# One core, attention and convolution in a decoder trunk: inverse root by logarithm and exponential, queries 512 wide, and the projection's weight subtractions one tile later

## The chip, the cores and the metric

The kernel runs on one core of one Trainium2 chip. The core has TensorE (PE, matrix products), VectorE (DVE), ScalarE (ACT), GpSimd (POOL) and the sync engine (SP), which here issues DMAs only; each works through its own list of instructions, and they wait for each other by semaphores. The metric is the device time of one execution in microseconds (us), as a median of runs.

## The reference

A trunk of two layers on 256 positions of width 1024. Each layer is half an FFN, a mixer, half an FFN; the mixer of layer 0 is a gated short convolution, that of layer 1 sparse attention with three branches on a shared K/V.

```python
def swiglu_ffn(x, w_in, w_out):
    gate, up = jnp.split(x @ w_in, 2, axis=-1)
    return (jax.nn.silu(gate) * up) @ w_out

def short_conv_mixer(x, w_in, conv_w, w_out):
    b_gate, c_gate, v = jnp.split(x @ w_in, 3, axis=-1)
    u = c_gate * v
    y = depthwise_causal_conv(u, conv_w)             # width 3
    return (b_gate * y) @ w_out

def nsa_mixer(x, w_q, q_norm, w_o, rel_bias, kv):
    proj = x @ w_q
    q = rmsnorm(proj[..., :1024] as 16 heads of 64, q_norm)
    gates = sigmoid(proj[..., 1024:])                # 3 per head
    # per head: o_c (compressed blocks), o_s (selected blocks), o_w (window), each
    # softmax(q @ k.T / 8 + rel_bias[bucket]) @ v with its own keys and mask
    out = gates[0] * o_c + gates[1] * o_s + gates[2] * o_w
    return out @ w_o

for i in range(2):
    if i == 1: kv = shared_kv(h, ...)
    h = h + 0.5 * swiglu_ffn(rmsnorm(h, ffn1_norm[i]), ...)
    h = h + mixer(rmsnorm(h, mix_norm[i]))
    h = h + 0.5 * swiglu_ffn(rmsnorm(h, ffn2_norm[i]), ...)
```

## The kernel before

**Split arithmetic.** Every product is made from halves: an operand is copied to a rounded type (its high half) and the rest is found by subtraction (its low half); high x high, high x low and low x high are added up in PSUM. For weights the class `Stream` does this. It loads 1 MB chunks by SP into `ws` (3 buffers); `high()` casts 1024 columns into `wh` on ACT (L148) and keeps them on a list; `low()` takes the oldest from that list and subtracts into `wl` on VectorE (L165). A unit (`wh`, `wl`) is free again after `done()`; six may be held. A chunk has two units, and a `ws` buffer is loaded anew when the low half of its second unit has been made.

**Stages.** The hidden state `h` lies in SBUF as 8 tiles of 128 x 256 (inside `base`). In turn come: FFN, convolution, FFN, K/V, FFN, attention, FFN. An FFN's first product works in groups of two column tiles: 16 matmuls of 512 columns (L322), then 16 of 256 (L325), from the inputs `xs`.

**The convolution's output projection** is `out_proj(zs, 1.0, nm)` with 8 input tiles, so its evacuation `out_evac` takes the `short` way. For each of the 8 output tiles c TensorE makes a product into one of 4 PSUM banks `a` (tiles 0 to 3 by L322/L325, tiles 4 to 7 by L434/L436); then VectorE adds it to `h[c]` (L394, twice), ACT scales it into the high half of the next stage's input (`norm.high`, L276), ACT squares it (`norm.squares`, L291) for POOL to add up (L293), and VectorE makes its low half (`norm.low`, L280), one tile later. Between them stand `W.high()` and `W.low()`, which prepare weights to come. After them follows the first group of the next FFN: tiles 0 to 5 of `xs`, then tile 6, then the row sums of the norm (L298, on the added squares), then tile 7.

**Attention** runs over 8 pairs of heads j, each with two heads g. The string `ORDER` is a program written out by hand: each word calls one function of the table `ops`, and each engine gets its instructions in the order of the words. `S_j` makes the scores (L1009) into both `mm` banks, `M_j_g` adds the bias and takes minima on VectorE (L1017), `E_j_g` exponentials on ACT (L1028), `R` reciprocals on VectorE, `N` the scaling on POOL (with `_d` on VectorE), `T` and `H` transposes on TensorE into a bank `a`, `C` and `CH` copies out of it on ACT (with `_d` on VectorE), `V_j` the product with the values and the compressed branch's weights, `O` and `P` its halves, `CM` to `CPC` the compressed branch, `WA` and `WD` weights' high and low halves, `WO` the output projection.

Queries come in two parts. Those of heads 0 to 7 are made ahead of the words. The later ones (`F`, 16 words) are made between the words as filler. In the kernel before they are two lots of 256 columns, q = 2 and 3; each is squared (`SQ`), summed and scaled (`RD`), brought to an inverse root by a bit trick and three Newton steps on VectorE (`NW`, L913 to L918), multiplied (`QM`), transposed (`QT`) and scaled (`QC`).

Of the kernel before, what the change touches and what calls it, by code (L numbers as in the profile page):

```python
# [44 lines left out]
F E_0_1 R_0_1 SQ_2 F RD_2 S_1 QT_1 E_0_0 F F QC_1 R_0_0 M_1_0 N_0_1 M_1_1 E_1_0 F S_2 NW_2 N_0_0 F CM_0 CX_0 F F E_1_1
R_1_0 N_1_0 CE_0 M_2_1 CR_0 QM_2 F E_2_1 R_1_1 CG_0 T_0_1 T_0_0 H_0 M_2_0 R_2_1 SQ_3 C_0_1 N_1_1_d E_2_0 S_3 QT_2
C_0_0 CI_0 N_2_1 CH_0_d CL_0 R_2_0 T_1_1 M_3_1 M_3_0 QC_2 C_1_1 T_2_1 CM_1 T_1_0 C_2_1 H_1 N_2_0 E_3_0 RD_3 CX_1 CH_1
C_1_0 CP_0 CPC_0 NW_3 S_4 CE_1 R_3_0 T_2_0 M_4_0 CR_1 N_3_0 M_4_1 CG_1 H_2 C_2_0 V_0 E_3_1 R_3_1 V_1 QM_3 E_4_0 R_4_0
# [11 lines left out]
def trunk(ctx, tc, A, out):  # L60
# [331 lines left out]
    def out_evac(o, c, factor, norm, short=False):  # L392
        for x in range(2):
            ve.scalar_tensor_tensor(out=h[c], in0=o[:, x * T:(x + 1) * T], scalar=factor, in1=h[c], op0=ALU.mult, op1=ALU.add)  # L394
# [498 lines left out]
    def q_reduce(q, tt, w):
        n = w // 64
        s = X["s"] if q == 0 else X.setdefault(("s", q), sm([P, 8])) if tt == 0 else X["s", q]
        ve.tensor_reduce(out=s[:, tt * n:tt * n + n], in_=X.pop(("sq", q, tt)).rearrange("p (n d) -> p n d", d=64), axis=AX.X, op=ALU.add)
        if tt:
            for a in range(2):
                z = s[:, a * n:a * n + n]
                ve.tensor_scalar(out=z, in0=z, scalar1=1.0 / 64, scalar2=X["s"][:, 18 + a:19 + a], op0=ALU.mult, op1=ALU.add)  # L900
# [8 lines left out]
    def q_newton(q):  # L909

        x = X.pop(("s", q))
        y, t = sm([P, 8]), sm([P, 8])
        ve.tensor_scalar(out=y.bitcast(I32), in0=x.bitcast(I32), scalar1=1, scalar2=None, op0=ALU.logical_shift_right)  # L913
# [7 lines left out]
    def q_normed(q, tt, w):  # L921

        n = w // 64
        X["q", q, tt] = t = t2([P, w])
        r = X["r", q][:, tt * n:tt * n + n].rearrange("p (g a) -> p g a", g=2)[:, :, :, None].to_broadcast([P, 2, n // 2, 64])
        ve.tensor_tensor(out=t.rearrange("p (a g d) -> p g a d", g=2, d=64),
                         in0=X["o", q][tt].rearrange("p (g a d) -> p g a d", g=2, d=64), in1=r, op=ALU.mult)
        if tt:
            del X["o", q]

    def q_trans(g):

        q, c0 = (0, g * T) if g < 2 else (g, 0)
# [11 lines left out]
    def later_queries():  # L945

        for q in (2, 3):
            o, us = bank([P, 2, T]), W.take(2)
            for tt in range(2):
                for k in range(8):  # L950
                    wh, wl = [us[k // 4][x][:, k % 4 * T:(k % 4 + 1) * T] for x in range(2)]
                    sh, sl = xs[k][:, tt * P:(tt + 1) * P], xs[k][:, T + tt * P:T + (tt + 1) * P]
                    pe.matmul(o[:, tt], sh, wh, start=(k == 0), stop=False)
                    pe.matmul(o[:, tt], sl, wh, start=False, stop=False)
                    pe.matmul(o[:, tt], sh, wl, start=False, stop=(k == 7))
                    if k == 7 and tt == 1:
                        W.done(2, False)
                        X["o", q] = [o[:, x] for x in range(2)]
                        del o
                    if k % 2 == 1:  # L960
                        yield

# [313 lines left out]
```

## Time and profile before

| | |
|---|---|
| median of 3 runs | 975.84 us (975.15 to 976.04) |
| the profiled execution | 976.69 us; 974.8 us from its first to its last instruction |
| granted clock of TensorE | 1.00 |
| TensorE, VectorE, ACT, POOL busy | 965.8, 735.4, 571.8, 126.4 us |
| from HBM | 175.57 MB, 181 GB/s over the span |
| the convolution's output projection | about 259 to 292 us |
| attention's words | about 708 to 776 us |

A row of a profile names the engine, the line of the kernel, the operation and the tiles, out<-in, without the buffers' numbers; a line can be that of a helper which many stages use. A matmul's duration runs to its modelled end, and the next one starts well before that, so the pace of matmuls is read from starts or from the chain, not from their durations. Idle time of an engine counts only where the chain passes through it.

### The profile page before, as it was taken

What the parts mean: (1) busy time and instruction counts of PE and PEld (TensorE: products, weight loads), DVE (VectorE), ACT (ScalarE), POOL (GpSimd) and SP (SyncE); (2) the same over time, 40 slices, a digit from 0 to 9 for tenths busy, and PEclk for the clock granted to TensorE, in tenths of its full rate; (3) what the DMA queues carried; (4) which work ended last, traced back from release to release, by engine and by line L of the source; (5) the groups of instructions that cost most, each with busy time, mean ns of one, the idle gap of its engine ahead of it and who ended that gap; (6) DMA issues with size and microseconds to landing.
All of it is one profiled execution on the core that took longest, in us unless ns stands there. A gap on an engine that the chain in (4) does not pass through costs nothing.

```text
span 974.8 us, 14677 instructions
## 1 busy us (share of the span) xinstructions
PE 965.8 (99%) x5662; PEld 845.1 (87%) x5662; DVE 735.4 (75%) x1180; ACT 571.8 (59%) x975; POOL 126.4 (13%) x208
## 2 busy tenths in 40 slices
PE   8999999999989999999999999999999999999998
PEld 7888888888878888888888888888887888888888
DVE  6889776578879878866549988866589888877752
ACT  6666654455566656644547676754479676656530
POOL 2000000044530000000111013000137210000000
PEclk9999999999999999999999999999999999999999
DMA  8556555545536875564544566555510356555550
GB/s 303 182 187 233 196 197 178 195 166 206 182 121 231 253 213 206 179 216 173 199 147 160 184 217 234 187 186 183 206 52 2 130 194 211 200 176 200 191 189 22
DMA packets 28433, 177.59 MB, mean 182 GB/s; under 512 B 3099, under 2 KB 6555, under 8 KB 7756
## 3 DMA queue, kind: packets, MB, share of 16 engines
q1 hardware_dynamic: 28364, 176.66, 53.0%
q8 instruction: 44, 0.72, 0.3%
q14 instruction: 25, 0.20, 0.1%
HBM read 175.57 MB, written 1.08 MB: 181 GB/s over the span
## 4 chain that ended last, share of the span: by engine, by line
PE 93%; ACT 3%; DVE 2%; DMA 1%; issue 1%; POOL 0%; SPq 0%; POOLq 0%
PE mm L322 35%; PE mm L325 18%; PE a L434 16%; PE a L436 9%; PE a L322 3%; PE a L325 2%; ACT pr L1028 1%; PE a L657 1%; PE a L659 1%; PE a L658 1%; PE a L1074 1%; DMA base<-in_first_dram 1%; ACT wh L148 1%; PE mm L1009 0%; DVE wl L474 0%
## 5 line engine op out<-in xcount | busy, mean ns | idle before, releaser
L165 DVE TENSOR_TENSOR wl<-ws,wh 128x1024 fp32r<-128x1024 f32 x318 | 390.0, 1241 | 103.9 <-PE a L436 63.0
L322 PE MATMUL mm<-xs,wh 128*128 128x512 f32 x1488 | 359.1, 392 | 1.7 <-DVE xs L280 1.5
L148 ACT CAST wh<-ws 128x1024 fp32r<-128x1024 f32 x318 | 328.1, 1044 | 38.0 <-PE a L434 19.6
L322 PEld LDWEIGHTS mm<-xs,wh 128*128 128x128 f32 x1488 | 273.0, 188 | 55.5 <-DVE xs L280 2.1
L325 PEld LDWEIGHTS mm<-xs,wl 128*128 128x128 f32 x1488 | 191.9, 191 | 8.0
L325 PE MATMUL mm<-xs,wl 128*128 128x256 f32 x1488 | 194.3, 283 | 0.0
L434 PE MATMUL a<-act,wh 128*128 128x512 f32 x714 | 169.2, 391 | 0.5 <-DVE base L394 0.5
L434 PEld LDWEIGHTS a<-act,wh 128*128 128x128 f32 x714 | 131.8, 188 | 26.7 <-issue 0.7
L335 DVE TENSOR_TENSOR t<-mm,t 128x512 f32<-128x512 f32 x95 | 65.4, 688 | 67.7 <-ACT t L334 66.8
L334 ACT COPY t<-mm 128x512 f32<-128x512 f32 x95 | 55.5, 585 | 91.2 <-PE mm L325 87.4
L436 PEld LDWEIGHTS a<-act,wl 128*128 128x128 f32 x714 | 90.6, 191 | 2.7
L436 PE MATMUL a<-act,wl 128*128 128x256 f32 x714 | 91.8, 283 | 0.0
L293 POOL TENSOR_TENSOR sq<-sq,t 128x256 f32<-128x256 f32 x35 | 29.3, 838 | 402.9 <-ACT t L291 402.8
L351 ACT ACTIVATE t<-t 128x256 f32<-128x256 f32 x88 | 36.8, 418 | 64.5 <-DVE t L339 64.4
L276 ACT ACTIVATE xs<-base 128x256 fp32r<-128x256 f32 x48 | 24.0, 505 | 83.6 <-DVE base L394 74.8
L339 DVE TENSOR_TENSOR t<-t,R 128x512 f32<-128x512 f32 x88 | 61.6, 700 | 2.6
L328 ACT CAST act<-t 128x256 fp32r<-128x256 f32 x96 | 39.0, 407 | 29.8 <-DVE t L587 19.4
L329 DVE TENSOR_TENSOR act<-t,act 128x256 fp32r<-128x256 f32 x96 | 40.9, 426 | 5.2 <-ACT act L328 5.2
L352 DVE TENSOR_TENSOR t<-t,t 128x256 f32<-128x256 f32 x88 | 36.8, 419 | 3.6 <-ACT t L351 3.5
L394 DVE SCALAR_TENSOR_TENSOR base<-a,base 128x256 f32<-128x256 f32 x78 | 32.8, 421 | 7.9 <-PE a L436 5.8
L280 DVE SCALAR_TENSOR_TENSOR xs<-base,xs 128x256 fp32r<-128x256 f32 x48 | 26.2, 549 | 11.7 <-ACT xs L276 11.6
L1028 ACT ACTIVATE pr<-pr,sm 128x128 f32<-128x128 f32 (+1 forms) x64 | 28.4, 463 | 1.1 <-DVE sm L1017 1.1
(258 smaller groups left out, 801.7 us busy)
## 6 DMA issues: line engine op xcount, KB each, us to landing
ws<-in_ffn_w_in_dram SPq DMA_DIRECT2D x85, 1024.0 KB, 4.9
ws<-in_ffn_w_out_dram SPq DMA_DIRECT2D x44, 1024.0 KB, 4.8
ws<-in_conv_w_in_dram SPq DMA_DIRECT2D x12, 1024.0 KB, 4.8
ws<-in_w_kv_dram SPq DMA_DIRECT2D x6, 1024.0 KB, 4.9
ws<-in_conv_w_out_dram SPq DMA_DIRECT2D x4, 1024.0 KB, 4.8
ws<-in_attn_w_q_dram SPq DMA_DIRECT2D x4, 1024.0 KB, 4.8
ws<-in_attn_w_o_dram SPq DMA_DIRECT2D x4, 1024.0 KB, 4.8
base<-row_d SPq DMA_DIRECT2D x8, 256.0 KB, 5.9
```

Source lines behind the costliest of these rows:

```text
L148: ac.copy(h, src)
L165: ve.tensor_tensor(out=l, in0=src, in1=h.bitcast(F32), op=ALU.subtract)
L322: pe.matmul(o, u[0][:, k * P:(k + 1) * P], xs[k], start=(k == 0), stop=False)
L325: pe.matmul(o[:, :T], u[1][:, k * P:(k + 1) * P], xs[k][:, :T], start=False, stop=(k == last))
L328: ac.copy(dst[:, :T], src)
L329: ve.tensor_tensor(out=dst[:, T:], in0=src, in1=dst[:, :T].bitcast(F32), op=ALU.subtract)
L334: ac.copy(r, o[:, :, T:])
L335: ve.tensor_tensor(out=r, in0=o[:, :, :T], in1=r, op=ALU.add)
L339: ve.tensor_tensor(out=r, in0=r, in1=R[:, None, :].to_broadcast([P, n, T]), op=ALU.mult)
L434: pe.matmul(o, run[k][0], lhs[k], start=(k == 0), stop=False)
L436: pe.matmul(o[:, :T], run[k][1], lhs[k][:, :T], start=False, stop=(k == n - 1))
L1028: ac.activation(pr[:, c0:c0 + w], pr[:, c0:c0 + w], AF.Exp, scale=-1.0, bias=mx[:, n:n + 1], accum_out=su[:, n:n + 1])
```

## The change

It has three parts.

In `out_evac`'s short way `norm.low(c - 1)` and `W.low()` move ahead of `W.high()`, and `W.low()` is called for c < 5 in place of c < 4. At tile 0 it finds an empty list and does nothing.

```diff
         norm.high(c)
+        if c:
+            norm.low(c - 1)
+        if c < 5:
+            W.low()
         W.high()
         norm.squares(c)
-        if c:
-            norm.low(c - 1)
-        if c < 4:
-            W.low()
         if c == ND - 1:
             norm.low(c)
```

The later queries are one lot of 512 columns: two banks, one for each half of the positions, 16 words `F` of one input tile each. Their inverse root is `exp(-0.5 * ln(x))` on ACT with one Newton step on VectorE. The word `exp` now loads a set of ACT's tables by its name, one that holds both functions: in ACT's list one table load stands there, as before, and none beside Ln and Exp.

```diff
     def q_newton(q):
         x = X.pop(("s", q))
-        y, t = sm([P, 8]), sm([P, 8])
-        ve.tensor_scalar(out=y.bitcast(I32), in0=x.bitcast(I32), scalar1=1, scalar2=None, op0=ALU.logical_shift_right)
-        ve.tensor_scalar(out=y.bitcast(I32), in0=y.bitcast(I32), scalar1=-1, scalar2=0x5f3759df, op0=ALU.mult, op1=ALU.add)
-        for _ in range(3):
-            ve.scalar_tensor_tensor(out=t, in0=y, scalar=-0.5, in1=y, op0=ALU.mult, op1=ALU.mult)
-            ve.tensor_tensor(out=t, in0=t, in1=x, op=ALU.mult)
-            ve.scalar_tensor_tensor(out=y, in0=t, scalar=1.5, in1=y, op0=ALU.add, op1=ALU.mult)
+        y, t = sm([P, 16]), sm([P, 16])
+        ac.activation(t, x, AF.Ln)
+        ac.activation(y, t, AF.Exp, scale=-0.5)
+        t = sm([P, 16])
+        ve.scalar_tensor_tensor(out=t, in0=y, scalar=-0.5, in1=y, op0=ALU.mult, op1=ALU.mult)
+        ve.tensor_tensor(out=t, in0=t, in1=x, op=ALU.mult)
+        ve.scalar_tensor_tensor(out=y, in0=t, scalar=1.5, in1=y, op0=ALU.add, op1=ALU.mult)
...
-        for q in (2, 3):
-            o, us = bank([P, 2, T]), W.take(2)
-            for tt in range(2):
-                for k in range(8):
-                    wh, wl = [us[k // 4][x][:, k % 4 * T:(k % 4 + 1) * T] for x in range(2)]
...
+        us = W.take(4)
+        X["o", 1] = []
+        for tt in range(2):
+            o = bank()
+            for k in range(8):
+                wh, wl = [us[k // 2][x][:, k % 2 * 512:(k % 2 + 1) * 512] for x in range(2)]
...
-        "exp": lambda: ac.activation(mk([P, 1], "warm", 1), epst, AF.Exp), "qn": lambda tt: q_normed(0, tt, 512),
+        "exp": lambda: ac.preload_act_table_set("natural_log_exp_and_others"), "qn": lambda tt: q_normed(0, tt),
```

The matmul of the compressed branch leaves `values` and gets a word of its own, `U`, which may stand before or after `V`; the first of the two takes the bank. With that the words are in a new order, of which two lines are shown.

```diff
+    def compressed(j):
+        o, first = summed(j)
+        pe.matmul(o, vc[:, j // 4].rearrange("p g d -> p (g d)"), ct.pop(j), start=first, stop=not first)
...
-GT qs_0 qr_0 F qs_1 F qr_1 GC F root F recip GA qn_0 qn_1 QT_0 exp WA_0 WD_0 QC_0 GX F S_0 GE GD M_0_1 F WA_1 M_0_0 F
+GT qs_0 F qs_1 qr_0 F F qr_1 GC root WA_0 exp recip qn_0 F qn_1 QT_0 QC_0 GA GX F GE S_0 GD WA_1 M_0_1 QT_1 M_0_0
```

What this makes of the engines' lists is shown at three places. The first is VectorE in the convolution's output projection, tiles 0 to 4, before and then after. `base<-a` is a product added to `h`, `xs` the next stage's input, `wl<-ws,wh` a subtraction of weights.

```order
L394 SCALAR_TENSOR_TENSOR base<-a_2607,base 128x256 x2
L165 TENSOR_TENSOR wl_2665<-ws_2568,wh_2662 128x1024
L394 SCALAR_TENSOR_TENSOR base<-a_2608,base 128x256 x2
L280 SCALAR_TENSOR_TENSOR xs_2598<-base,xs_2598 128x256
L165 TENSOR_TENSOR wl_2680<-ws_2568,wh_2672 128x1024
L394 SCALAR_TENSOR_TENSOR base<-a_2609,base 128x256 x2
L280 SCALAR_TENSOR_TENSOR xs_2599<-base,xs_2599 128x256
L165 TENSOR_TENSOR wl_2693<-ws_2590,wh_2687 128x1024
L394 SCALAR_TENSOR_TENSOR base<-a_2610,base 128x256 x2
```

```order
L394 SCALAR_TENSOR_TENSOR base<-a_2607,base 128x256 x2
L394 SCALAR_TENSOR_TENSOR base<-a_2608,base 128x256 x2
L280 SCALAR_TENSOR_TENSOR xs_2598<-base,xs_2598 128x256
L165 TENSOR_TENSOR wl_2671<-ws_2568,wh_2662 128x1024
L394 SCALAR_TENSOR_TENSOR base<-a_2609,base 128x256 x2
L280 SCALAR_TENSOR_TENSOR xs_2599<-base,xs_2599 128x256
L165 TENSOR_TENSOR wl_2686<-ws_2568,wh_2673 128x1024
L394 SCALAR_TENSOR_TENSOR base<-a_2610,base 128x256 x2
```

The subtraction of the first weights (`wh_2662`) stood after tile 0's addition and stands after tile 1's; every later one has moved by a tile too, so that its `wh` is a tile old.

The second place is the later queries' inverse root. Before, on VectorE, the chain of lot 2, between the second `M` of pair 1 and the minima of the compressed branch (L1092):

```order
L913 TENSOR_SCALAR sm_7038<-sm_6962 128x8
L914 TENSOR_SCALAR sm_7038<-sm_7038 128x8
L916 SCALAR_TENSOR_TENSOR sm_7039<-sm_7038 128x8
L917 TENSOR_TENSOR sm_7039<-sm_7039,sm_6962 128x8
L918 SCALAR_TENSOR_TENSOR sm_7038<-sm_7039,sm_7038 128x8
L916 SCALAR_TENSOR_TENSOR sm_7039<-sm_7038 128x8
L917 TENSOR_TENSOR sm_7039<-sm_7039,sm_6962 128x8
L918 SCALAR_TENSOR_TENSOR sm_7038<-sm_7039,sm_7038 128x8
L916 SCALAR_TENSOR_TENSOR sm_7039<-sm_7038 128x8
L917 TENSOR_TENSOR sm_7039<-sm_7039,sm_6962 128x8
L918 SCALAR_TENSOR_TENSOR sm_7038<-sm_7039,sm_7038 128x8
L1092 TENSOR_REDUCE sm_7062<-t_1177_6914 128x8
```

After, on VectorE and then on ACT, after the last `M` of pair 2 (line numbers are those of the changed kernel; L1061 is a copy, L1025 an exponential):

```order
L896 TENSOR_REDUCE sm_6956<-t_1205_7048 128x8
L900 TENSOR_SCALAR sm_6956<-sm_6956,sm_6810 128x8 x2
L916 SCALAR_TENSOR_TENSOR sm_7089<-sm_7085 128x16
L917 TENSOR_TENSOR sm_7089<-sm_7089,sm_6956 128x16
L918 SCALAR_TENSOR_TENSOR sm_7085<-sm_7089,sm_7085 128x16
L1029 RECIPROCAL sm_7043<-sm_7043 128x4
L925 TENSOR_TENSOR t_1220_7109<-a_6830,sm_7085 128x2x4x64
L925 TENSOR_TENSOR t_1221_7112<-a_6934,sm_7085 128x2x4x64
```

```order
L891 ACTIVATE t_1205_7048<-a_6934 128x512
L1061 COPY xs_7053<-a_7030 128x512
L1061 COPY xs_7077<-a_7060 128x512
L1124 CAST cs_6742<-t_1199_7017 128x16x16
L913 ACTIVATE sm_7086<-sm_6956 128x16
L914 ACTIVATE sm_7085<-sm_7086 128x16
L1061 COPY xs_7099<-a_7080 128x512
L1025 ACTIVATE pr_7065,sm_7126<-pr_7065,sm_7066 128x128 x2
```

Two chains of eleven on VectorE have become one of three, with two activations on ACT (L913, L914) between VectorE's scaling (L900) and its step (L916).

The third place is TensorE at the first words `F`, before and after:

```order
L953 MATMUL a_6831<-wh_6737,xs_6209 128x256
L954 MATMUL a_6831<-wh_6737,xs_6209 128x256
L955 MATMUL a_6831<-wl_6739,xs_6209 128x256
L953 MATMUL a_6831<-wh_6737,xs_6210 128x256
L954 MATMUL a_6831<-wh_6737,xs_6210 128x256
L955 MATMUL a_6831<-wl_6739,xs_6210 128x256
```

```order
L953 MATMUL a_6830<-wh_6737,xs_6209 128x512
L954 MATMUL a_6830<-wh_6737,xs_6209 128x512
L955 MATMUL a_6830<-wl_6739,xs_6209 128x512
L953 MATMUL a_6830<-wh_6737,xs_6210 128x512
L954 MATMUL a_6830<-wh_6737,xs_6210 128x512
```

One word held two input tiles of 256 columns and now holds one of 512; there are 16 words in both.

More of the change, by code (lines that the diff above doesn't have):

```diff
@@ L43 @@
 ORDER = """
-GT qs_0 qr_0 F qs_1 F qr_1 GC F root F recip GA qn_0 qn_1 QT_0 exp WA_0 WD_0 QC_0 GX F S_0 GE GD M_0_1 F WA_1 M_0_0 F
[L45 to L48, printed above, removed]
@@ new lines @@
+C_0_0 S_3 QM_0 CL_0 QM_1 M_3_1 T_1_1 E_2_0 CP_0 M_3_0 CH_0 CPC_0 QT_2 QC_2 C_1_1 N_2_1 E_3_0 H_1 QT_3 R_2_0 T_2_1
+CH_1_d S_4 QC_3 E_3_1 CM_1 N_2_0 V_0 C_2_1_d R_3_0 M_4_0 M_4_1 T_2_0 CX_1 U_0 U_1 H_2 N_3_0 O_0 P_0 R_3_1 CE_1 CR_1
+C_2_0_d N_3_1 E_4_1 S_5 CG_1 V_1 T_3_1 CH_2 M_5_1 E_4_0 R_4_1 T_3_0 M_5_0 H_3 CH_3_d CI_1 CM_2 S_6 C_3_1_d N_4_1 E_5_1
+O_1 T_4_1 CL_1 R_4_0 C_3_0_d R_5_1 CP_1 P_1 M_6_1 WA_2 CX_2 CE_2 CR_2 CPC_1_d V_3 E_6_1 V_2 C_4_1 N_4_0 T_4_0 M_6_0
+C_4_0_d U_3 H_4 CG_2 E_5_0 CI_2 E_6_0 CH_4_d N_5_1 R_5_0 N_5_0_d U_2 S_7 CL_2 O_2 CP_2 CPC_2 V_4 O_3 U_4 O_4 WA_3
@@ L931, in q_trans @@
     def q_trans(g):
[L933 removed]
+        q, c0 = g // 2, g % 2 * T
         X["qt", g] = pb = bank([P, 2, T])
@@ L945, in later_queries @@
     def later_queries():
-        for q in (2, 3):
-            o, us = bank([P, 2, T]), W.take(2)
-            for tt in range(2):
-                for k in range(8):
-                    wh, wl = [us[k // 4][x][:, k % 4 * T:(k % 4 + 1) * T] for x in range(2)]
[L952 to L961, printed above, removed]
+        us = W.take(4)
[4 more added lines that the diff above has]
+                wh, wl = [us[k // 2][x][:, k % 2 * 512:(k % 2 + 1) * 512] for x in range(2)]
+                sh, sl = xs[k][:, tt * P:(tt + 1) * P], xs[k][:, T + tt * P:T + (tt + 1) * P]
+                pe.matmul(o, sh, wh, start=(k == 0), stop=False)
+                pe.matmul(o, sl, wh, start=False, stop=False)
+                pe.matmul(o, sh, wl, start=False, stop=(k == 7))
+                if k == 7:
+                    X["o", 1].append(o)
+                    W.done(4 * tt, False)
+                yield
     def g_sum():
@@ L1065, in copied, with summed @@
         X["p", *key[1:]] = t
+    def summed(j):
+        first = ("v", j) not in X
+        if first:
+            X["v", j] = bank([P, T])
+        return X["v", j], first
+    def compressed(j):
+        o, first = summed(j)
+        pe.matmul(o, vc[:, j // 4].rearrange("p g d -> p (g d)"), ct.pop(j), start=first, stop=not first)
     def values(j):
-        pp, o = j // 4, bank([P, T])
+        pp, (o, first) = j // 4, summed(j)
         lo, hi = [X.pop(("p", j, g2)) for g2 in range(2)], X.pop(("p", j))
@@ L1073, in values @@
                 rows, c0 = slice(g2 * 64, g2 * 64 + 64), b * 256 + (2 * pp + g2) * 64
-                pe.matmul(o[rows], V[0][:, c0:c0 + 64], lo[g2][:, b], start=(b == 0), stop=False)
+                pe.matmul(o[rows], V[0][:, c0:c0 + 64], lo[g2][:, b], start=(first and b == 0), stop=False)
         for b in range(2):
@@ L1077, in values @@
                 rows, c0 = slice(g2 * 64, g2 * 64 + 64), b * 256 + (2 * pp + g2) * 64
-                pe.matmul(o[rows, P:], V[1][:, c0:c0 + 64], hi[:, g2, b], start=False, stop=False)
-        pe.matmul(o, vc[:, pp].rearrange("p g d -> p (g d)"), ct.pop(j), start=False, stop=True)
-        X["v", j] = o
+                pe.matmul(o[rows, P:], V[1][:, c0:c0 + 64], hi[:, g2, b], start=False, stop=(b == 1 and not first))
     def out_hi(j):
@@ L1157, in trunk @@
         "CH": lambda j, e="": copied(("t", j), act([P, 2, 2, P], F32), copy[e]),
-        "V": values, "O": out_hi, "P": out_lo,
+        "U": compressed, "V": values, "O": out_hi, "P": out_lo,
         "CM": c_min, "CX": c_less, "CE": c_exp, "CR": c_recip, "CG": c_gate, "CI": c_high, "CL": c_low, "CP": c_trans,
```

37 lines of the change are left out of this document (17 added, 20 removed).

## Prediction

> **What bounds the kernel now.** I read the page's first lines and the chain, then the waits of TensorE, then the timeline at the two places that the change touches: 256 to 300 us (output projection of the convolution) and 707 to 776 us (attention).
>
> ```profile
> span 974.8 us, 14677 instructions
> ...
> PE 965.8 (99%) x5662; PEld 845.1 (87%) x5662; DVE 735.4 (75%) x1180; ACT 571.8 (59%) x975; POOL 126.4 (13%) x208
> ...
> PE 93%; ACT 3%; DVE 2%; DMA 1%; issue 1%; POOL 0%; SPq 0%; POOLq 0%
> ```
> ```profile
> PE mm L322 <- DVE xs L280: 1.5, 2, 0.9
> ...
> PE a L298 <- POOL sq L293: 0.5, 1, 0.5
> PE a L434 <- DVE base L394: 0.5, 1, 0.5
> ```
>
> TensorE is the bound nearly everywhere: 93% of the chain, and busy 99% of the span. So the kernel gets shorter only where TensorE waits or where it gets less to do. The three waits above (total us, times, longest) all lie in one place, the output projection of the convolution. There the timeline (start, duration, engine, line, tiles; in brackets the idle time before the row and what ended it) reads:
>
> ```profile
> 276.15 2.00 PE L434 MATMUL a<-act,wh 128*128 128x512 f32 x8
> 276.36 1.03 ACT L148 CAST wh<-ws 128x1024 fp32r<-128x1024 f32 x1
> ...
> 277.42 1.23 DVE L165 TENSOR_TENSOR wl<-ws,wh 128x1024 fp32r<-128x1024 f32 x1 [1.12 <-ACT wh L148]
> ...
> 277.85 1.39 POOL L293 TENSOR_TENSOR sq<-sq,t 128x256 f32<-128x256 f32 x1 [2.14 <-ACT t L291]
> ...
> 278.56 0.88 DVE L394 SCALAR_TENSOR_TENSOR base<-a,base 128x256 f32<-128x256 f32 x2
> 279.35 0.47 DVE L280 SCALAR_TENSOR_TENSOR xs<-base,xs 128x256 fp32r<-128x256 f32 x1
> 279.47 0.51 ACT L276 ACTIVATE xs<-base 128x256 fp32r<-128x256 f32 x1 [1.76 <-DVE base L394]
> ...
> 279.58 2.09 PE L434 MATMUL a<-act,wh 128*128 128x512 f32 x8 [0.48 <-DVE base L394]
> 279.88 1.03 ACT L148 CAST wh<-ws 128x1024 fp32r<-128x1024 f32 x1
> ...
> 280.95 1.22 DVE L165 TENSOR_TENSOR wl<-ws,wh 128x1024 fp32r<-128x1024 f32 x1 [1.12 <-ACT wh L148]
> ...
> 282.09 0.88 DVE L394 SCALAR_TENSOR_TENSOR base<-a,base 128x256 f32<-128x256 f32 x2
> ...
> 283.51 0.47 PE L322 MATMUL mm<-xs,wh 128*128 128x512 f32 x1 [0.19 <-ACT xs L276]
> ...
> 284.60 0.50 PE L322 MATMUL mm<-xs,wh 128*128 128x512 f32 x1 [0.63 <-DVE xs L280]
> ...
> 285.97 1.90 PE L322 MATMUL mm<-xs,wh 128*128 128x512 f32 x7 [0.87 <-DVE xs L280]
> ...
> 289.32 0.41 ACT L291 ACTIVATE t<-base 128x256 f32<-128x256 f32 x1
> ...
> 289.87 1.08 POOL L293 TENSOR_TENSOR sq<-sq,t 128x256 f32<-128x256 f32 x1 [0.92 <-ACT t L291]
> ...
> 291.00 0.70 PE L298 MATMUL a<-sq,ones 128*128 128x256 f32 x2 [0.52 <-POOL sq L293]
> ...
> 292.24 3.80 PE L322 MATMUL mm<-xs,wh 128*128 128x512 f32 x16
> ```
>
> The reader is to see a ring between two engines. L394 of one output tile (278.56) lets ACT scale it (L276, 279.47), behind which ACT makes the next weights' high half (L148, 279.88); VectorE's subtraction (L165, 280.95) waits 1.12 us for that, and the next L394 stands behind it (282.09). One turn is 282.09 - 278.56 = 3.53 us. VectorE falls behind TensorE, tile 7's product waits for a PSUM bank (279.58), the first FFN group waits for its inputs (283.51, 284.60, 285.97), and the row sums L298 wait for the last square (291.00).
>
> **Change 1: the subtractions one tile later.** VectorE now subtracts the weights whose high half ACT made a tile earlier: same instructions, same number (four, after tiles 1 to 4 and no longer 0 to 3). A turn on VectorE is then its own work, 0.88 + 0.47 + 1.23 = 2.58 us; on ACT 0.51 + 1.03 + 0.41 = 1.95 us. TensorE's tile is 8 matmuls of 512 and 8 of 256 columns; with their pace from
>
> ```profile
> 292.40 3.64 PE mm L322 x16
> ...
> 296.04 1.91 PE mm L325 x16
> ```
>
> (3.64/16 = 0.228 us, 1.91/16 = 0.119 us) it is 2.78 us. So TensorE becomes the slowest of the three. Tiles count from 0, and the row at 278.56 is tile 3's. The first subtraction still follows the first cast and stays where it is; what stands behind it is now L394 of tile 2 and no longer that of tile 1, at 278.56 - 2 x 3.53 = 271.5. From there the turns give tile 3 at 274.1, tile 4 at 276.7, tile 5 at 279.2 and, without a subtraction after tile 5, tile 6 at 280.6. Tile 7's bank is that of tile 3, free at 275.0: its product starts at 276.15 + 2.78 = 278.9 instead of 279.58 and ends at 281.7. The group's matmul on tile 5 comes 5 x 0.228 later, at 282.8; VectorE has tile 5 ready after L394 of tile 6 (281.5) and one L280, at 282.0. Tile 7's L394 runs from 281.9 to 282.8, its scaling on ACT to 283.3 and its L280 to 283.8, long before its turn at the end of the group.
>
> What a group costs with rows of a norm in its midst and no wait is read where it stands after attention:
>
> ```profile
> 787.19 2.91 PE L322 MATMUL mm<-xs,wh 128*128 128x512 f32 x12
> ...
> 793.20 3.80 PE L322 MATMUL mm<-xs,wh 128*128 128x512 f32 x16
> ```
>
> 6.01 us. Here two matmuls for the bias table are added (2 x 0.228). The next group would start at 281.7 + 6.01 + 0.46 = 288.2 instead of 292.24: 4.0 us less. I take 3.9. The last square is the other thing that could be late. On ACT it stands behind the cast of tile 7 (283.3 + 1.03 + 0.41 = 284.8), and POOL's addition then ends at 285.9 (1.08 us at 289.87) or 286.2 (1.39 us at 277.85, the longest of the rows shown). L298 wants it after 12 x (0.228 + 0.119) + 2 x (0.228 + 0.119) + 0.46 = 5.3 us of the group, at 287.0.
>
> Moved past whom: the weight loads on SP wait for a stage buffer that the subtractions free, and none of these comes later than before: the first stays, the second starts at 271.5 + 0.88 + 0.47 = 272.9 against 280.95 - 2 x 3.53 = 273.9, the third at 275.5 against 277.42, the fourth at 278.1 against 280.95. Nothing is queued behind a later load. After 292 TensorE is saturated at 5.56 us a group and no row of VectorE or ACT waits for it there, so what is won stays won. Lower end: only the bank wait and two of the input waits go (0.48 + 0.63 + 0.87 = 2.0 us); upper end 4.0.
>
> **Change 2: attention.** Its rows:
>
> ```profile
> 707.90 2.02 PE L968 MATMUL a<-xs,wh 128*96 128x512 f32 x8
> ...
> 743.76 0.66 PE L1060 MATMUL a<-small,pr 128*128 128x128 f32 x4 [0.34 <-ACT act L941]
> ```
> ```profile
> 776.02 2.00 PE L322 MATMUL a<-act,wh 128*128 128x512 f32 x8
> ```
> ```profile
> 730.00:740.00 10.00, 9.94 (x87) 7.17 (x83) 9.56 (x59) 10.00 (x37) 6.95 (x18) 1.00 0.01 2
> ```
> ```profile
> 710.32 0.22 ACT L903 ACTIVATE sm<-sm 128x18 f32<-128x18 f32 x1
> ```
> ```profile
> 716.01 0.29 DVE L1017 CUSTOM_DVE_ANT_0 pr<-base,mm 128x128 f32<-128x128 f32 x1 [0.37 <-PE mm L1009]
> ...
> 718.41 0.17 DVE L1032 RECIPROCAL sm<-sm 128x4 f32<-128x4 f32 x1
> ...
> 719.41 0.89 DVE L900 TENSOR_SCALAR sm<-sm,sm 128x4 f32<-128x4 f32 x2
> ...
> 723.23 0.16 DVE L913 TENSOR_SCALAR sm<-sm 128x8 int32<-128x8 int32 x1
> ...
> 725.32 0.28 DVE L1092 TENSOR_REDUCE sm<-t 128x8 f32<-128x128 f32 x1
> ```
> ```profile
> 737.31 3.50 ACT pr L1028 x16
> ```
>
> The stage lasts 68.1 us (707.90 to 776.02) and TensorE has one wait in it that the profile names, 0.34 us. In a slice of 10 us (span, then PE, PEld, DVE, ACT, POOL) TensorE is busy 9.94, ACT 10.00 and VectorE 9.56: three engines have no room, so a new order may win or lose little.
>
> TensorE: 96 matmuls of 256 columns become 48 of 512, 96 x 0.119 - 48 x 0.228 = 11.46 - 10.94 = 0.5 us less. Splitting the compressed branch's matmul (U) off the values keeps its number. The Trainium skill, TensorE: Matmul & The Clock Gate, Back-to-back issue gap, gives 262 and 518 cycles at 2.4 GHz, 109 and 216 ns. By those the term would be 0.1 us and the time 0.4 us longer; the trace's 0.119 and 0.228 decide.
>
> VectorE: two Newton chains of 11 instructions (723.23 to 725.32, 2.09 us each) become one of three, at 0.19 each: 4.18 - 0.57 = 3.6 us less; the scalings at L900 are half as many (0.9 us less). Most of it lies beside TensorE's work, which no row shows waiting for these; where it comes onto the path is the ring below. ACT: Ln and Exp on 128x16 are new, at 0.22 each by L903, its nearest row; the table load changes its name and place, not its number.
>
> The new wait is a round trip: VectorE's reduction and scaling, ACT's Ln and Exp, VectorE's step. Behind it on VectorE stand R_2_1, the two QM, M_3_1 and M_3_0; for these TensorE's CP_0 (its bank is that of the queries), QT_2 and S_4 wait. I walked the new order by hand with the durations above (an E word on ACT is 3.50/2 = 1.75 us, an M word on VectorE (718.41 - 716.01)/2 = 1.2). Up to S_3 TensorE waits some 0.4 us, at T_0_0, whose bank ACT must empty while the queries hold two of the four; the round trip makes S_4 wait another 0.2 to 0.5; after that only waits of 0.1 to 0.3 remain, and ACT is never idle. The losses add up to about 0.9, the gains are 0.5 and the 0.34 at 743.76: attention comes out even, within 1 us either way.
>
> **Sum.** The profiled execution took 976.69 us (span 974.8), 0.85 above the median of 975.84. 976.69 - 3.9 + 0.0 = 972.8; against the median 971.9 us.
>
> **Rivals.** (a) Attention gains as well: the 0.9 us of losses in my walk are not there and some 0.6 us of gaps between words go too: 971.9 - 1.5 = 970.4. For it: VectorE has 4.5 us less to do where it is 9.56 of 10 busy. Against: ACT has as much as before at 10.00 of 10. (b) The convolution's gain is halved: the first turns stay a tile behind, or the last addition on POOL, behind ACT's cast, comes after 287.0; the row sums wait and only 2.0 us are won: 973.8. Against: margins of about 1 us, 282.0 before 282.8 and 286.2 before 287.0. That the change does nothing at all would need L165 to wait for L148 still, though that cast then is a whole tile old; I give it 2 in 100. (c) Attention loses 1 to 3 us: 973 to 975. (d) Slower than before: ACT becomes the bound of attention. Every microsecond in which ACT stands still between the first and the last exponential, above all at Ln, which waits for VectorE, then moves the end; the price is 1 us for 1 us, and it decides from 3.9 us of such waiting on, where my walk finds 0.3. It would give 976 to 979.
>
> **How the numbers follow.** Forecast 0.58 (own range 970.9 to 973.0), (a) 0.16, (b) with no effect 0.12, (c) 0.10, (d) 0.04. The range goes from 970.3, most of (a), to 974.0, (b) and half of (c). A measurement of this kernel tells about 0.2%, 1.95 us, from no change: faster means below 973.9. Forecast, (a), half of (b) and half of (c) lie there, 0.85; the rest of (b) and (c) within, 0.11; (d) 0.04.
>
> **What would show it.** Right: L165 in the projection without idle time before it from tile 2 on, L394 every 2.8 us, no wait at tile 7, L298 ending within 0.3 us of TensorE's own pace, FFN groups 3.5 to 4 us earlier, and attention's distance from L968 to the first tile with a full product 67 to 69 us. Wrong: L298 still named with POOL, L280 still named for L322, or ACT idle at Ln by more than 1 us with S_4 late.

## The result and the profile after

The changed kernel takes 969.50 us (median of 6 runs, 969.29 to 970.05) against 975.94 us (6 runs, 975.15 to 976.24): ratio 0.9936, 95% interval 0.9923 to 0.9949. Forecast were 971.9 us and a range from 970.3 to 974.0. The direction and the convolution's term came as forecast. The time lies 2.4 us below the forecast and 0.8 below the range: attention, put at 0.0, gained 2.10 and lost 0.45 behind it, and some 0.6 of the 2.4 no stretch of the trace shows (below).

The page of the profiled execution (969.29 us), its first lines and the chain that ended last:

```profile
span 967.5 us, 14556 instructions
...
PE 962.2 (99%) x5614; PEld 842.1 (87%) x5614; DVE 730.8 (76%) x1152; ACT 570.6 (59%) x972; POOL 128.6 (13%) x213
...
PE 97%; DVE 1%; DMA 1%; ACT 1%; issue 0%; SPq 0%
```

TensorE's share of the chain rose from 93% to 97%. Of the waits of TensorE, L280, L298 and L434 in the convolution are gone; two remain behind the kernel's first microseconds, both in or behind attention (us in total, times, longest):

```profile
PE a L1051 <- ACT xs L1061: 0.4, 1, 0.4
PE mm L322 <- DVE xs L280: 0.2, 1, 0.2
```

The timeline of the convolution's output projection; first the row with which the first FFN group begins in the kernel before, then the changed kernel:

```profile
282.46 0.86 PE L322 MATMUL mm<-xs,wh 128*128 128x512 f32 x3
```

```profile
268.76 1.23 DVE L165 TENSOR_TENSOR wl<-ws,wh 128x1024 fp32r<-128x1024 f32 x1 [0.33 <-ACT wh L148]
...
269.90 0.88 DVE L394 SCALAR_TENSOR_TENSOR base<-a,base 128x256 f32<-128x256 f32 x2
...
271.09 1.77 DVE L165 TENSOR_TENSOR wl<-ws,wh 128x1024 fp32r<-128x1024 f32 x1
...
272.78 0.87 DVE L394 SCALAR_TENSOR_TENSOR base<-a,base 128x256 f32<-128x256 f32 x2
...
275.10 0.88 DVE L394 SCALAR_TENSOR_TENSOR base<-a,base 128x256 f32<-128x256 f32 x2
...
277.35 2.00 PE L434 MATMUL a<-act,wh 128*128 128x512 f32 x8
...
277.67 0.87 DVE L394 SCALAR_TENSOR_TENSOR base<-a,base 128x256 f32<-128x256 f32 x2
...
280.14 2.91 PE L322 MATMUL mm<-xs,wh 128*128 128x512 f32 x12
...
283.80 1.10 POOL L293 TENSOR_TENSOR sq<-sq,t 128x256 f32<-128x256 f32 x1 [0.91 <-ACT t L291]
...
285.49 0.59 PE L298 MATMUL a<-sq,ones 128*128 128x256 f32 x2
...
286.63 1.08 PE L322 MATMUL mm<-xs,wh 128*128 128x512 f32 x4
```

Only the first L165 still waits for its cast (0.33 us); from then on VectorE turns without a pause, tile 7's product (277.35) follows at once, and the group that cost 9.78 us with its waits (282.46 to 292.24) takes 6.49 us (280.14 to 286.63). With the 1.59 us by which the changed kernel started sooner (next table), the group begins 0.73 us earlier and is 3.29 shorter: 4.02 us.

**Where the 6.4 us are.** TensorE sets the pace of this kernel, so the trace is divided at the starts of its rows: the first L322, the first matmul of attention (L968 before, L965 after), the first FFN tile with a full product behind attention (776.02 and 768.31), and the end of the span. The profiles of all runs were divided alike; five of them:

| kernel | to first L322 | to attention | attention | behind it | span | median, us |
|---|---|---|---|---|---|---|
| before | 24.65 | 683.25 | 68.12 | 198.74 | 974.76 | 975.94 |
| changed | 23.06 | 679.23 | 66.02 | 199.20 | 967.50 | 969.50 |
| before, run again | 23.60 | 683.26 | 68.13 | 198.73 | 973.72 | 976.12 |
| convolution's edit alone | 23.79 | 679.23 | 68.11 | 198.73 | 969.86 | 971.56 |
| attention's edits alone | 24.31 | 683.22 | 66.01 | 199.18 | 972.73 | 973.97 |

The three stretches repeat within 0.05 us from profile to profile, where the code in them is the same, and can be read to that. The start, the same code in all, took 23.06 to 24.65 us in 17 profiles. A transfer of `base` stands in its chain, before and then after:

```profile
2.11 5.78 DMA base<-in_first_dram
```
```profile
2.11 5.00 DMA base<-in_first_dram
```

It landed at 7.89 and 7.11 us, in the 17 profiles at 6.75 to 8.03, and mostly the start was longer the later it landed. The two profiles that are compared here are the two ends of the start, so 1.59 us of the 7.26 between their spans are no effect of the change. What is: 4.02 in the convolution, 2.10 in attention, 0.45 lost behind it, 5.67 in all. The medians differ by 6.44, 0.77 more. Part of that goes with the clock: of before's 75 runs taken beside the experiments, 40 show a granted clock of 0.998 and have a median of 976.38 us, 33 show 1.00 and have 975.69, while all 52 runs of kernels with the convolution's edit show 0.999 or 1.00. Against before at 1.00 the gain is 6.2 us; the 0.5 that is left lies within what the start does from run to run. Why the clock differs is open.

### The profile page after: what moved, and what is told of

It reads as the page before. It is cut to its first block, busy times and chain, and to the rows that moved or that the text cites. A ratio compares the mean times of both kernels' runs of the same rounds, so it can differ in the third digit from the quotient of the medians.

```text
span 967.5 us, 14556 instructions
## 1 busy us (share of the span) xinstructions
PE 962.2 (99%) x5614; PEld 842.1 (87%) x5614; DVE 730.8 (76%) x1152; ACT 570.6 (59%) x972; POOL 128.6 (13%) x213
## 4 chain that ended last, share of the span: by engine, by line
PE 97%; DVE 1%; DMA 1%; ACT 1%; issue 0%; SPq 0%
PE mm L322 36%; PE mm L325 19%; PE a L434 17%; PE a L436 9%; PE a L322 2%; PE mm L1006 1%; PE a L325 1%; PE a L657 1%; PE a L659 1%; PE a L658 1%; PE mm L480 1%; PE a L1083 1%; PE a L1051 1%; DVE wl L165 1%; DMA base<-in_first_dram 1%; PE a L480 0%
## 5 line engine op out<-in xcount | busy, mean ns | idle before, releaser
L165 DVE TENSOR_TENSOR wl<-ws,wh 128x1024 fp32r<-128x1024 f32 x318 | 391.3, 1245 | 98.1 <-PE a L436 63.0
L322 PE MATMUL mm<-xs,wh 128*128 128x512 f32 x1488 | 358.6, 392 | 0.2 <-DVE xs L280 0.2
L322 PEld LDWEIGHTS mm<-xs,wh 128*128 128x128 f32 x1488 | 273.1, 188 | 53.4 <-DVE xs L280 0.6
L434 PE MATMUL a<-act,wh 128*128 128x512 f32 x714 | 169.1, 391 | 0.0
L434 PEld LDWEIGHTS a<-act,wh 128*128 128x128 f32 x714 | 131.9, 188 | 26.0
L335 DVE TENSOR_TENSOR t<-mm,t 128x512 f32<-128x512 f32 x95 | 65.4, 688 | 66.7 <-ACT t L334 65.8
L293 POOL TENSOR_TENSOR sq<-sq,t 128x256 f32<-128x256 f32 x35 | 26.9, 768 | 398.3 <-ACT t L291 398.1
L394 DVE SCALAR_TENSOR_TENSOR base<-a,base 128x256 f32<-128x256 f32 x78 | 32.7, 421 | 8.1 <-PE a L436 6.1
L280 DVE SCALAR_TENSOR_TENSOR xs<-base,xs 128x256 fp32r<-128x256 f32 x48 | 24.5, 514 | 11.9 <-ACT xs L276 11.9
L1025 ACT ACTIVATE pr<-pr,sm 128x128 f32<-128x128 f32 (+1 forms) x64 | 28.3, 448 | 2.0 <-DVE sm L1014 2.0
```

The costliest lines, as they stand in the source:

```text
L165: ve.tensor_tensor(out=l, in0=src, in1=h.bitcast(F32), op=ALU.subtract)
L322: pe.matmul(o, u[0][:, k * P:(k + 1) * P], xs[k], start=(k == 0), stop=False)
L335: ve.tensor_tensor(out=r, in0=o[:, :, :T], in1=r, op=ALU.add)
L434: pe.matmul(o, run[k][0], lhs[k], start=(k == 0), stop=False)
```

## The experiments

### Each half alone

Two kernels: before with the hunk of the convolution, and the changed kernel without that hunk.

> The kernel before with the convolution's edit alone. Theory 1 (the two changes add, the convolution's is worth what the walk of its rows gave): 975.9 - 4.0 = 971.9 us, the stretch from the first L968 to the first FFN tile with a full product 68.1 us as before. Rival (the convolution's edit carries the surplus too, or attention needs it): 969.5 to 971, with all of 6 us from here.

> The changed kernel with the convolution's projection put back as it was. Theory 1 (attention gains by itself): the stretch from the first L965 to the first FFN tile with a full product is 66.0 us against 68.1, the time 975.9 - 1.65 = 974.3; if the rest of the 6.4 us belongs to the code too, 973.5. Prediction as put: attention even, 975.9. A gain over 2.5 us (below 973.4) would mean that the two edits don't add.

Measured: 971.56 us (ratio 0.9956, 0.9942 to 0.9970) and 973.97 us (0.9980, 0.9972 to 0.9989). The rows of the table: the convolution's edit gives 4.02 us and touches nothing else; attention's edits give 2.10 and lose 0.45 behind, with the convolution as before. The halves add to 0.02 us. Before run again, unchanged, shows what a measurement of nothing looks like:

> The kernel before, unchanged, for the start: from the span's start to the first L322 it took 24.65 us in the first profile of before, 24.31, 23.79, 23.42, 23.20 and 23.06 in five others with the same code there. Theory (what the transfers of the first 20 us do from run to run): ratio 1.000 within 0.001, and a start anywhere from 23.0 to 24.7. Rival (the program of before starts slower for good): 24.6 again.

976.12 against 975.92 us, ratio 1.0002 (0.9993 to 1.0011), start 23.60: the long start of before's first profile was chance.

### What in attention gained: TensorE's words

The times between one matmul's start and the next one's, summed over the rows of the trace by word (V with both its lines, L1074 and L1078 before; "rest" is the WO parts), in us:

| kernel | F | S | T, H | V | U | GT, GX, QT, CP | rest | attention |
|---|---|---|---|---|---|---|---|---|
| before | 12.10 | 12.86 | 11.82 | 11.61 | 2.33 | 6.04 | 11.36 | 68.12 |
| changed | 11.68 | 12.61 | 11.15 | 11.16 | 1.80 | 6.14 | 11.48 | 66.02 |
| U joined to V again | 11.68 | 12.67 | 11.53 | 12.44 | 2.07 | 6.17 | 11.47 | 68.03 |
| before, U behind pairs of V | 12.11 | 13.06 | 12.23 | 11.00 | 1.55 | 6.13 | 13.49 | 69.56 |
| before, U ahead of pairs of V | 12.10 | 12.87 | 11.61 | 11.00 | 2.51 | 6.13 | 11.51 | 67.73 |
| changed, root by shift and three steps | 11.68 | 12.91 | 11.87 | 11.16 | 1.80 | 6.22 | 11.47 | 67.11 |

F falls by 0.42, but V and U, the same matmuls in both kernels, fall by 0.98 together. In the changed kernel's trace a V word lasts 0.05 longer behind a T than behind another V, its second half 0.10 longer ahead of a U than ahead of a V, and a U 0.31 ahead of a V but 0.22 ahead of a T. V works on 64 columns of the array and S on 64 rows; T, H, CP, QT, U and F work on all of it. Going through attention in the order of the rows, TensorE changes between these three forms 31 times before and 24 times after. A probe measured such a change by itself.

```
for a, b in ((full, cols), (full, rows), (cols, rows), (comp, cols), (full, comp)):
    grouped(a, b)      # 16 of a, then 16 of b
    mixed(a, b)        # eight times: two of a, two of b
```

> The changed kernel with a probe of 320 matmuls ahead of the last FFN, whose results nothing uses; its time means nothing, its rows do. For five pairs of forms, 16 of each in two blocks (one change of form) and then in turns of two (15 changes): full 128x128 transposes with 64-column matmuls, full with 64-row matmuls, 64-column with 64-row, compressed (128x128, fp32r) with 64-column, full f32 with compressed. Theory 1 (a change between the full array and a half costs about 0.1 us, in each direction): the turns last 14 x 0.1 = 1.4 us longer than the blocks for the first, second and fourth pair, and no longer for the third and fifth. Rival A (the slow places in attention are waits for data, not the form): no difference in any pair. Rival B (the type matters, fp32r against f32): the fourth and fifth pair alone.

The timeline of TensorE in the probe (L1185 full transposes, L1188 64 columns, L1191 64 rows, L1194 compressed; a matmul of f32 on half the array leaves two records, so x4 is two matmuls):

```profile
768.39 1.91 PE L1185 MATMUL a<-small,V 128*128 128x128 f32 x16
770.23 3.67 PE L1188 MATMUL a<-V,V 128*64 128x256 f32 x32
...
774.79 0.44 PE L1185 MATMUL a<-small,V 128*128 128x128 f32 x2
775.16 0.65 PE L1188 MATMUL a<-V,V 128*64 128x256 f32 x4
775.74 0.44 PE L1185 MATMUL a<-small,V 128*128 128x128 f32 x2
...
787.00 0.44 PE L1185 MATMUL a<-small,V 128*128 128x128 f32 x2
787.37 0.70 PE L1191 MATMUL a<-V,V 64*128 64x256 f32 x4
788.00 0.44 PE L1185 MATMUL a<-small,V 128*128 128x128 f32 x2
...
802.27 0.65 PE L1188 MATMUL a<-V,V 128*64 128x256 f32 x4
802.86 0.70 PE L1191 MATMUL a<-V,V 64*128 64x256 f32 x4
803.49 0.44 PE L1188 MATMUL a<-V,V 128*64 128x256 f32 x2
...
817.70 0.50 PE L1194 MATMUL a<-act,vc 128*128 128x256 f32 x2
818.13 0.65 PE L1188 MATMUL a<-V,V 128*64 128x256 f32 x4
818.72 0.50 PE L1194 MATMUL a<-act,vc 128*128 128x256 f32 x2
...
829.54 0.38 PE L1185 MATMUL a<-small,V 128*128 128x128 f32 x2
829.68 0.49 PE L1194 MATMUL a<-act,vc 128*128 128x256 f32 x2
830.00 0.38 PE L1185 MATMUL a<-small,V 128*128 128x128 f32 x2
```

Inside the blocks a transpose starts every 0.109 us and a pair of half-array records every 0.216, so two and two take 0.65 us without a change. In turns, full and 64 columns take 0.95 (774.79 to 775.74), full and 64 rows 1.00 (787.00 to 788.00): 0.15 and 0.175 a change. 64 columns and 64 rows take 1.22 (802.27 to 803.49) against 0.87: 0.18 a change, where theory 1 had expected none. The compressed matmul, which works on the full array in fp32r, takes 1.01 in turns with 64 columns (817.70 to 818.72) against 0.67: 0.17 a change. Full f32 and full fp32r take 0.46 (829.54 to 830.00), as in blocks: the type costs nothing. So it is the form, every change of it, also from one half to the other. The Trainium skill, TensorEngine Tiling (Array Packing), Key Properties, says that a change of the tiling mode, unlike a change of the tile, drains TensorE; it gives no figure, and the probe agrees with it at 0.15 to 0.18 us. Seven changes fewer are then 1.05 to 1.26 us. Of attention's 2.10 us, 0.42 of F and 1.05 to 1.26 of form leave 0.4 to 0.6 us, by subtraction, for waits that are gone; S's rows show 0.25 of it.

### Taking the parts back

The 512-wide matmuls as two of 256:

> The changed kernel with each of the 48 later-query matmuls of 512 columns as two of 256. The term of the prediction (96 x 0.119 against 48 x 0.228): 0.5 us longer, 970.0, the stretch of attention 66.5 us. Rival (those matmuls are not on the path, or the gap is the 0.1 us of the cycle counts): 969.5 to 969.6.

Attention 66.46, 0.44 more (forecast 0.5). The cycle counts of the Trainium skill, TensorE: Matmul & The Clock Gate, Back-to-back issue gap, had given 0.1; the trace disagrees. The median, 970.56 us, is 1.06 above the changed kernel's; the trace has 0.44 of it.

U put right behind its V in the changed order:

> The changed kernel with each compressed word U put right behind its V, as before the change. Theory 1 (TensorE pays about 0.095 us each time it goes from a full 128x128 word to one on half of the array and again on the way back; three more such blocks, V_2 and V_3 apart and V_5, V_6, V_7 apart): 6 x 0.095 = 0.57 us longer, 970.1 us, the stretch of attention 66.6 us. Rival (what attention gained is VectorE's relief or fewer waits, the place of U is nothing): 969.5 and 66.0.

971.67 us, attention 68.03, 2.01 more: the direction of theory 1, over three times its size. The form changes went up to 30, six more, 0.9 to 1.1 us; and a wait came that the place of U had avoided (line numbers are one higher in this kernel):

```profile
PE a L1075 <- DVE act L1139: 0.8, 1, 0.8
```

U needs the copy CPC, V does not. In the changed order every U comes when its copy is ready: the view of its waits lists no U.

In the kernel before, U split from V and put behind each pair of V, and in a second kernel ahead of it:

> The kernel before with nothing changed but U: split from V and put behind the second V of each pair (V_0 V_1 U_0 U_1 and so on; O_4 and O_6 follow their U). Newton chains, 256-wide queries and every other word stay. Theory 1 (cost of leaving and re-entering the half-array words): four times V 0.91, Vh 0.54, U 0.31, V 0.91, Vh 0.54, U 0.31 becomes V 0.91, Vh 0.44, V 0.86, Vh 0.54, two U 0.32 to 0.42, 0.35 less each, 1.4 in all: attention 66.7 to 67.0 us against 68.1, time 974.7. Rival (VectorE's relief or the rest of the order made the gain): 68.1 and 976.0.

> The kernel before with U split from V and put AHEAD of each pair (U_0 U_1 V_0 V_1 and so on), so that no O word comes later than before (U and U and V end before V and U did) and TensorE changes its form 23 times instead of 31. Theory 1 (each change 0.15 us, on the path when nothing becomes late by it): V, Vh and U 1.2 to 1.4 us less, attention 66.8 to 67.3 us against 68.1, time 0.9 to 1.3 below before. Rival (in the old order ACT and VectorE hold attention, so TensorE's saving comes back as waits whatever the place): 68.0 to 68.3, ratio 1.000.

Behind the pairs V and U took 1.39 us less, as theory 1 said (1.4), and the kernel became slower all the same: 977.55 us, ratio 1.0014 (1.0005 to 1.0023), attention 69.56. The O and P words came later, and what stands behind them. Two waits are new, that of a T word for a reciprocal (L1033), which comes 1.06 us later than before, counted from attention's start, and that of the last projections for P (L1098):

```profile
PE a L1055 <- DVE sm L1033: 0.8, 1, 0.8
...
PE mm L323 <- DVE act L1098: 0.6, 1, 0.6
```

Ahead of the pairs hardly anything behind is late (the WO parts by 0.15 us), V is as short (11.00), but U itself waits (2.51 against 1.55), now for the copies that empty a bank:

```profile
PE a L1078 <- ACT xs L1065: 0.3, 1, 0.3
```

Attention 67.73, 0.39 less, 975.85 us, ratio 0.9999 (0.9990 to 1.0008): not measurable. Both theories were half right. The form's price is real on TensorE, and in the old order most of it came back as waits.

### The root

The changed kernel with shift and three Newton steps on 128x16, and before with Ln, Exp and one step:

```
-ac.activation(t, x, AF.Ln)
-ac.activation(y, t, AF.Exp, scale=-0.5)
+ve.tensor_scalar(..., op0=ALU.logical_shift_right)
+ve.tensor_scalar(..., scalar2=0x5f3759df, ...)
 (one step  ->  three steps)
```

> The changed kernel with the inverse root again by shift and three Newton steps on VectorE, once for 128x16, in place of Ln, Exp and one step: 8 more instructions on VectorE (8 x 0.19 = 1.5 us), 2 fewer on ACT, no round trip. Theory 1 (attention's gain is TensorE's own and this work lies beside it): attention 65.8 to 66.3 us, time 969.3 to 969.8. Rival (VectorE's relief carries the gain): 67.5 and 971.0.

> The kernel before with the two later queries' roots taken by Ln, Exp and one Newton step instead of shift and three steps; same words, 256-wide queries, U with V. VectorE has 2 x 8 x 0.19 = 3.0 us less, ACT 4 x 0.22 = 0.9 us more, two round trips are new. Theory 1 (VectorE's relief reaches the path: the rewritten kernel lost 1.1 us of attention when it was taken back): attention 67.0 to 67.6 us, time 975.0 to 975.6. Rival (in the old order ACT holds attention and the round trips cost what VectorE wins): 68.1 to 68.6, time 976.0 to 976.5.

In the new order the old root costs: 971.49 us, attention 67.11, 1.09 more, against theory 1. The timeline where it comes onto the path; first the kernel with the old root, then the changed kernel (the first lies 0.82 later by attention's start):

```profile
726.93 1.29 DVE L925 TENSOR_TENSOR t<-a,sm 128x512 f32<-128x512 f32 x2
...
727.76 0.63 PE L1134 MATMUL a<-small,cs 128*128 128x128 f32 x4 [0.53 <-POOL pr L1043]
```
```profile
723.71 0.24 ACT L913 ACTIVATE sm<-sm 128x16 f32<-128x16 f32 x1
...
724.23 0.17 DVE L916 SCALAR_TENSOR_TENSOR sm<-sm 128x16 f32<-128x16 f32 x1 [0.67 <-ACT sm L914]
...
724.85 1.29 DVE L925 TENSOR_TENSOR t<-a,sm 128x512 f32<-128x512 f32 x2
...
726.25 0.60 PE L1134 MATMUL a<-small,cs 128*128 128x128 f32 x4
...
728.77 1.65 PE L1006 MATMUL mm<-kt,act 64*128 64x288 f32 x12
```

The two QM (L925) start 1.26 us later, CP_0 on TensorE (L1134) waits 0.53 us, and S_4's word lasts 1.88 us (730.36 to 732.23) instead of 1.58 (728.77 to 730.34). CP_0 takes a bank that the queries hold until QM. POOL, which the row names, isn't what it needs: its input from POOL was done at 725.19, the first QM at 727.62. In the changed kernel VectorE stands idle 0.67 us for the round trip and still is done earlier; ACT comes to Ln (L913) without idle time, and S_4 (728.77) starts without a wait. In the old order the same edit gives nothing: 976.16 us, ratio 1.0001 (0.9992 to 1.0010), attention 68.44, 0.32 more. What the new root is worth, minus 0.3 or plus 1.1, is set by the order around it.

### Tries for a faster kernel

Two words moved in the changed order, then four more (V_4 to S_7, C_0_1 ahead of SQ_1; V_3 V_2 to S_7 too):

> The changed kernel with two words moved: V_4 right behind S_7 (ahead of CP_2), so that TensorE changes its form twice there and not three times (0.15 us, by the probe 0.150 to 0.175 a change), and C_0_1 ahead of SQ_1 on ACT, so that T_0_0's bank comes free some 0.6 us earlier. Theory 1 (TensorE's time and that wait are on the path): 0.15 plus up to 0.4 less, attention 65.4 to 65.9 us against 66.0, time 968.9 to 969.4. Rival (the waits come back elsewhere, as after U was paired in the kernel before; SQ_1 later makes the queries later): 66.0 to 66.6, 969.5 to 970.

> As the run before, and V_3 V_2 moved down to stand right ahead of S_7 V_4, with U_3 U_2 behind: four changes of form instead of six by then (0.3 to 0.35 us less than the run before has there... against the changed kernel three changes, 0.45 to 0.5 us). Theory 1: attention 65.1 to 65.7 us, time 968.6 to 969.2. Rival (O_2, O_3, P_2, P_3 and the last projections come later, as after U was paired in the kernel before): 66.2 to 67.5, 969.7 to 971.

971.28 us (attention 67.49) and 972.41 us (68.82): in both the rival's direction, and more than the rival said. V_4 had covered the copy of CP_2 for U_4, which now waits 0.7 us for it. C_0_1 moved ahead only to wait for its own T word; the squares (L892) that had filled that time came behind it. ACT and TensorE in the first of the two:

```profile
723.72 0.59 ACT L1062 COPY xs<-a 128x512 f32<-128x512 f32 x1 [0.50 <-PE a L1052]
724.21 0.61 ACT L892 ACTIVATE t<-a 128x512 f32<-128x512 f32 x1
724.45 0.63 PE L1052 MATMUL a<-small,pr 128*128 128x128 f32 x4 [0.33 <-ACT xs L1062]
...
725.34 0.66 PE L1058 MATMUL a<-small,pr 128*128 128x128 f32 x4 [0.26 <-ACT xs L1062]
```

So the 0.38 us at T_0_0 is a round trip from TensorE to ACT and back, which the copy's earlier place didn't take away.

Last, the 0.45 us behind attention. Attention now ends with fewer WO parts behind the first complete bank, so VectorE begins the last tiles (L1191, L1184 before) 1.21 us ahead of the first full product; before, 3.66 (before, then changed):

```profile
772.36 1.68 DVE L1184 TENSOR_TENSOR base<-mm,base 128x256 f32<-128x256 f32 x4
```
```profile
767.10 1.67 DVE L1191 TENSOR_TENSOR base<-mm,base 128x256 f32<-128x256 f32 x4 [1.98 <-PE mm L325]
...
768.31 1.99 PE L322 MATMUL a<-act,wh 128*128 128x512 f32 x8
...
780.97 1.87 PE L322 MATMUL mm<-xs,wh 128*128 128x512 f32 x7 [0.18 <-DVE xs L280]
```

Three kernels move the subtractions (`if 0 < c < 5` becomes `1 < c < 6`; the same with V_4 at S_7 and U_4 behind T_5_0; `0 < c < 4` with the fourth after the last tile):

> The changed kernel with the subtractions of attention's last tiles one tile later (after tiles 2 to 5, no longer 1 to 4), the same edit as in the convolution. In the changed kernel the stretch from the first full tile behind attention to the end takes 199.2 us, 0.45 more than before, and VectorE is without a pause from 770.65 to the first FFN group. Theory 1 (that chain of VectorE makes the 0.45): 198.75, time 969.05. Rival (TensorE's pace or a later wait makes it): 199.2 and 969.5, or more if the second subtraction is then missed by the first group.

> As the run before, and V_4 right behind S_7 with U_4 (and O_4) behind T_5_0, so that CP_2's copy has V-free cover of one T word: one change of form fewer, 0.15 us. Theory 1: attention 65.85 to 65.95 us, the rest 198.75, time 968.9. Rival (the copy CPC_2, 0.59 us on ACT, is late for U_4 again as in the run with two words moved): attention 66.1 to 66.7.

> The changed kernel with the fourth subtraction of attention's last tiles taken out of the chain (after tiles 1 to 3 as before, the fourth behind the last L280, ahead of the FFN's own). Theory 1 (VectorE's chain from the first to the eighth L1191 is what makes the first FFN group 0.45 us late; one L165 is 1.22 us of it): no wait and no stretching at the group, the stretch behind attention 198.75 to 198.85 us against 199.20 (199.07 with the subtractions one tile later, where one still stood ahead of the last tiles), time 969.1. Rival (something else in that stretch): 199.1 to 199.2 and 969.5.

One tile later: 969.68 us, 199.07 behind attention, 0.13 of the 0.45 back; the time is the changed kernel's. With V_4 at S_7: 971.02, attention 67.22, more than its rival's 66.1 to 66.7, since T_5_0 now waits for the bank that CPC_2 empties:

```profile
PE a L1052 <- ACT act L1139: 0.7, 1, 0.7
```

With the fourth subtraction out of the chain the first FFN group starts and runs as before the change (its twelve matmuls take 2.91 us, as at 787.19 in before), and then needs that very subtraction:

```profile
780.22 2.91 PE L322 MATMUL mm<-xs,wh 128*128 128x512 f32 x12
...
784.71 0.98 PE L325 MATMUL mm<-xs,wl 128*128 128x256 f32 x6 [0.87 <-DVE wl L165]
```

970.41 us, 199.85 behind attention, where theory 1 had 198.75 to 198.85. And in the kernel with the probe, whose 65 us of matmuls stand ahead of the first full product and let VectorE begin early, the stretch behind is 198.74, as before the change. So VectorE's chain of L1191, L280 and L165 is what makes the 0.45, and its late start the cause; moving a subtraction within it moves the wait. No kernel tried here beats the changed one by more than a measurement tells.

## Why the prediction was wrong in size and right in place

- **Convolution, 3.9: right (4.02).** With 1.59 us for the start added back, the walked times came within 0.3 us: L394 of tiles 2 to 6 forecast at 271.5, 274.1, 276.7, 279.2 and 280.6, seen at 271.49, 274.37, 276.69, 279.26 and 280.45; tile 7's product 278.9 and 278.94; the group 281.7 and 281.73; the next group 288.2 and 288.22. All signs named for this part were seen but one: L394 came every 2.3 to 2.9 us (tiles 2 to 5), not every 2.8. The last addition came at 286.5 instead of 286.2, still ahead of L298 at 287.1.
- **Attention, 0.0: wrong (2.10 gained, 0.45 lost behind it; the stretch of 66.02 us lies outside the 67 to 69 that were named as a sign).** The step that failed is the sum of gains 0.5 and 0.34 against losses of about 0.9. Two of its terms were wrong, each by about 1 us. The first was put at nothing: "Splitting the compressed branch's matmul (U) off the values keeps its number" was true and was taken for a price of nothing. It stands for seven changes of form, 1.05 to 1.26 us, of which V and U show 0.98 in the words. The second is the losses: with the 0.34 they were to make waits 0.6 us longer, and by the subtraction above they became 0.4 to 0.6 us shorter. The wait at T_0_0 came as walked (0.4; 0.38). The 0.2 to 0.5 at S_4 did not: the round trip holds VectorE 0.67 us and TensorE not at all, because VectorE's shorter chain more than pays for it, as the kernel with the old root shows (1.09 us). Of the small waits of 0.1 to 0.3 the view of waits lists none; from start to start one QT is 0.2 longer than the one before it. S has 0.25 us less of gaps than before. F was right: 0.5 forecast, 0.42 to 0.44 measured.
- **Behind attention:** the prediction has no term for what follows attention. 0.45 us of the gain went into VectorE's chain at the last tiles, which the new order starts 2.45 us later.
- **Rivals.** (a), attention gains too, is what happened, at 1.65 instead of 1.5 net, and that the two sizes agree is in part luck. It had the losses that aren't there, and VectorE's relief as the reason, which is the part of the cause that the kernel with the old root shows; the changes of form, the other part, are not in it. (d), ACT as the bound at Ln, was not seen: ACT has no idle time ahead of Ln (723.71).
- **What the kernels leave open.** The root's 1.09 is not a further term beside F, form and waits: it is what the old root would bring back in waits in the new order. The same goes for U's 2.01, of which only 0.9 to 1.1 is form. Which words of the new order won the 0.4 to 0.6 us of waits isn't shown; that would need kernels with one part of the order moved at a time.

## What to carry to other kernels

Count how often TensorE changes between the full array and its halves, and try to set words of one form side by side; price each change by a row, since the number of matmuls doesn't show it. A saving on the engine that bounds the kernel counts only if what is moved for it makes nothing late: of six reorderings by hand here, one gained 0.39 us in attention and five lost 1.2 to 2.8. Divide the trace at a few starts of the bounding engine and compare the stretches: they repeat to hundredths of a microsecond where whole runs scatter by 1 to 2 us.
